# Adding two decay tiles with an accumulating transfer instead of a VectorE instruction

## The chip, the core and the metric

The kernel runs on one core of one Trainium2 chip. The core has engines with an instruction queue each: TensorE (PE, matrix products, its weight loads shown as PEld), VectorE (DVE), ScalarE (ACT), GpSimd (POOL) and SyncE (SP), which here only issues transfers. An engine takes its instructions in order; an instruction that waits for something holds up all that stands behind it on that engine. Transfers run on 16 DMA engines that all issuers share. The metric is the device time of one execution in microseconds (us), lower is better. Before the change the median of three runs is 1244.33 us (1241.67 to 1247.54).

## What is computed

The reference is one layer of a hybrid block over 512 latent tokens of width 1024, with a context of 256 tokens. An input projection feeds a convolution branch and a bidirectional state-space mixer (Mamba-2, chunked scan with chunks of 128 tokens, 32 heads in 8 groups of 4, state 128), the branches are gated and projected, and a squared-ReLU MLP follows. What matters here is the part of the scan inside a chunk, once forwards and once on the flipped sequence:

```python
cum = jnp.cumsum(dts * a, axis=2)
seg = cum_t[..., :, None] - cum_t[..., None, :]
decay = jnp.exp(jnp.where(lower, seg, -jnp.inf))
cb = jnp.einsum('bcqgn,bckgn->bcgqk', cs_, bs)
y_diag = jnp.einsum('bcgrqk,bckgrp->bcqgrp', cb[:, :, :, None] * decay, xdt)
...
y = y_f + flip(y_b) + lp['ssm_d'][:, None] * xs
```

Both directions multiply the same product `cb` of C and B, so the kernel adds the forward decay (a lower triangle) and the backward decay (an upper triangle) of a head first, and multiplies the sum by `cb` once.

## The kernel before

Weights arrive as 128x1024 tiles `raw` (three buffers, SP issues them, L100); ACT rounds each to `whi` (L109) and DVE makes the rest `wlo` (L110). A projection tile is 24 matmuls of 512 columns (L118 to L120: three products for each of 8 slices). The program has an opening (norms, modulation, first projections), the scan stage with a loop over the 8 groups, and then gates, output projections and the MLP.

In the scan stage `ssd(g)` does the scan of group g while `proj(g + 1)` computes the next group's B, C, X and Z tiles, and for the first five groups a GLU tile and its 31-tap convolution on DVE (`taps`, L601) is mixed in. The list of instructions on each engine is fixed when the program is built: a list scheduler takes instructions by priority and by its own estimate of when each operand is ready, so an operation that moves to another engine moves others as well.

Per head, `expo` (L450) makes the summed decay two heads ahead of its use. For each direction it loads one row of cumulated sums from DRAM (`s_cf`), spread over 128 partitions, into a tile E of 128x512 float32 (L459, issued by SP, 256 KB); POOL masks one triangle (L463, affine select); ACT exponentiates in four pieces (L466). The forward tile comes from a pool with seven buffers and is freed when PE has used the product. The backward tile comes from tag "M" with three buffers; its last reader is the addition of both tiles (L468), which frees it for the backward tile of three heads later. DVE multiplies the sum by `cb` (L551), and PE uses it in the third part of `yps` (L560). The first two parts of `yps` (L564) need C times the decay from the chunk's start: tiles Cd, loaded by SP (L482) and multiplied on POOL, one in four on DVE (L483), and the states `hst`, which DVE steps from chunk to chunk (L541, L542) out of `sps` products (L529) of `xw` (L514). Then DVE forms `yt` (L568, L569), ACT stores it and squares it, and POOL sums the squares (`yacc`, L574).

SP's one queue thus carries the weights, the E rows and the Cd rows, in the scheduler's order.

Of the kernel before, what the change touches and what calls it, by code (L numbers as in the profile page):

```python
# [12 lines left out]
ALU = mybir.AluOpType  # L13
# [47 lines left out]
def build(tc, xT, ctxT, cond, crow, wada1, wada2, vecs, hv, cst, w_in, w_co, w_so, w_o, w_1, w_2, outT):  # L61
    nc = tc.nc
    with ExitStack() as es:
# [386 lines left out]
        def expo(upto):  # L450

            while asked[0] < min(upto, HEADS):
                h = asked[0]
                asked[0] += 1
                es_ = []
                for d in range(2):
                    hd = d * HEADS + h
                    e = (tp if d else spool).tile([P, T], F32, name="E", tag="M" if d else "E", bufs=3 if d else EB)
                    nc.sync.dma_start(e, s_cf[hd, 0].unsqueeze(0).broadcast_to([P, T]))  # L459

                    x3 = e.rearrange("p (c q) -> p c q", q=P)
                    sign = -1 if d else 1
                    nc.gpsimd.affine_select(x3, x3, pattern=[[0, NCH], [sign, P]], compare_op=ALU.is_ge,  # L463
                                            fill=never, base=0, channel_multiplier=-sign)
                    for c in range(NCH):
                        nc.scalar.activation(x3[:, c], x3[:, c], AF.Exp, bias=bT[:, c, hd:hd + 1])  # L466
                    es_.append(e)
                nc.vector.tensor_tensor(es_[0], es_[0], es_[1], ALU.add)  # L468
                ahead.append(es_[0])

        def ssd(g, Bt, Ct, X, Z):
# [72 lines left out]
            for j in range(2):  # L544
# [4 lines left out]
                for r in range(2):  # L549
                    M = ahead.pop(0)  # L550
                    nc.vector.tensor_tensor(M, M, cb, ALU.mult)  # L551
                    Ms.append(M)
                expo(4 * g + 2 * j + 2 + LEAD)
                for k in range(3):
                    for c in range(NCH):
# [53 lines left out]
        conv = first_xbc[0]  # L609
        cur = proj(0)  # L610
        expo(2)
        for g in range(G):
            ssd(g, *cur)
# [289 lines left out]
```

## Time and profile before

| | |
|---|---|
| median of the runs | 1244.33 us (1241.67 to 1247.54) |
| the profiled execution's own time | 1247.21 us |
| its span, first to last instruction | 1245.4 us |
| granted TensorE clock, mean | 0.991 |
| busy: PE, DVE, ACT, POOL | 1202.5, 919.3, 565.8, 166.7 us |
| E tiles loaded, additions of two E tiles | 64, 32 |

Busy time is the time in which an engine has an instruction running; the share over the whole span mixes stages that differ, so the stages are read apart. A wait is listed with the engine and line that waits, the one that ended it, the sum in us, how often, and the longest. In a timeline a row is start, duration, engine, line, operation, and how many instructions were merged; SPq and ACTq are transfers as they are issued. "To landing" is the time from the issue of a transfer to its arrival. L468 runs only in the scan stage, between 115.9 and 528.5 us of the span.

### The profile page before, as it was taken

Reading aid. Unit: us, or ns where it says so; the run is one execution under the profiler, and the core shown is the slowest. Engines: PE = TensorE matmul, PEld = TensorE weight load, DVE = VectorE, ACT = ScalarE, POOL = GpSimd, SP = SyncE. Lnnn points to the kernel's source line nnn. Section 1 sums busy time; section 2 is a strip of 40 time slices with the busy share of each in tenths; the row PEclk is TensorE's granted clock in tenths of the full one; section 3 lists DMA queues with packets and bytes.
Section 4 is the critical chain, followed back from the end, with each engine's and each line's share of the span. In section 5 each row is a group of like instructions: output and inputs, shape, how many; then the busy total and the mean of one; then the engine's idle time right before and its main releaser. Section 6 shows DMA issues by size and latency. Waiting matters only on the chain.

```text
span 1245.4 us, 17389 instructions
## 1 busy us (share of the span) xinstructions
PE 1202.5 (97%) x6662; PEld 996.3 (80%) x6662; DVE 919.3 (74%) x1426; ACT 565.8 (45%) x916; POOL 166.7 (13%) x138
## 2 busy tenths in 40 slices
PE   6998999999999999999999999999999999999997
PEld 3787778788888887787887878789988888888886
DVE  6797889999999989866999698877733343443454
ACT  4557877465564635342453561234422332322342
POOL 0003725042242424120010000000000000000000
PEclk8999999999999999999999999999999999999998
DMA  9427853443525352422363468956013332332322
GB/s 366 159 65 162 259 156 125 126 147 101 186 85 178 105 167 76 126 78 94 111 184 111 128 201 282 315 165 193 35 44 92 102 92 95 102 91 96 102 85 68
DMA packets 65331, 169.83 MB, mean 136 GB/s; under 512 B 7648, under 2 KB 10464, under 8 KB 65120
## 3 DMA queue, kind: packets, MB, share of 16 engines
q1 hardware_dynamic: 62944, 164.53, 42.1%
q10 hardware_dynamic: 2304, 4.20, 0.9%
q8 instruction: 52, 0.85, 0.3%
q14 instruction: 31, 0.25, 0.1%
HBM read 162.14 MB, written 6.55 MB: 135 GB/s over the span
## 4 chain that ended last, share of the span: by engine, by line
PE 64%; DVE 11%; DMA 9%; ACT 3%; issue 2%; POOL 0%; SPq 0%; DVEq 0%; POOLq 0%; ACTq 0%
PE ps L118 19%; PE ps L120 19%; PE ps L119 19%; DVE conv L601 3%; DMA E<-s_cf 3%; DMA Cd<-s_cf 3%; PE sps L529 2%; DMA aw<-in_wada_dram 2%; DVE wlo L110 2%; ACT E L466 2%; PE yps L564 2%; DMA yr<-s_y 1%; DVE Xt L381 1%; DVE Ct L381 1%; DVE Cd L483 1%
## 5 line engine op out<-in xcount | busy, mean ns | idle before, releaser
L109 ACT CAST whi<-raw 128x1024 fp32r<-128x1024 f32 x163 | 170.9, 1049 | 349.7 <-PE ps L119 304.4
L110 DVE TENSOR_TENSOR wlo<-raw,whi 128x1024 fp32r<-128x1024 f32 x163 | 202.2, 1241 | 97.5 <-ACT whi L109 89.0
L120 PE MATMUL ps<-hh,wlo 128*128 128x512 f32 x632 | 255.7, 405 | 4.2 <-DVE wlo L110 4.2
L118 PE MATMUL ps<-hh,whi 128*128 128x512 f32 x632 | 255.3, 404 | 3.2 <-DVE Ct L381 2.4
L119 PE MATMUL ps<-hl,whi 128*128 128x512 f32 x632 | 253.9, 402 | 0.0
L601 DVE SCALAR_TENSOR_TENSOR conv<-sg,V,conv 128x392 f32<-128x392 f32 (+14 forms) x240 | 177.2, 755 | 2.2
L120 PEld LDWEIGHTS ps<-hh,wlo 128*128 128x128 f32 x632 | 118.8, 188 | 33.9 <-DVE wlo L110 8.6
L118 PEld LDWEIGHTS ps<-hh,whi 128*128 128x128 f32 x632 | 118.8, 188 | 30.1 <-issue 5.9
L119 PEld LDWEIGHTS ps<-hl,whi 128*128 128x128 f32 x632 | 119.0, 188 | 25.3 <-issue 1.4
L738 DVE SCALAR_TENSOR_TENSOR x<-ps,mod,x 128x512 f32<-128x512 f32 (+1 forms) x48 | 31.6, 661 | 98.8 <-PE ps L120 98.8
L466 ACT ACTIVATE E<-E,bT 128x128 f32<-128x128 f32 x256 | 81.6, 394 | 34.3 <-POOL E L463 34.1
L120 PE MATMUL ps<-h2h,wlo 128*128 128x512 f32 (+1 forms) x240 | 89.9, 376 | 0.0
L119 PE MATMUL ps<-h2l,whi 128*128 128x512 f32 (+1 forms) x240 | 89.7, 375 | 0.0
L118 PE MATMUL ps<-h2h,whi 128*128 128x512 f32 (+1 forms) x240 | 89.7, 376 | 0.0
L119 PE MATMUL ps<-gl,whi 128*128 128x512 f32 x224 | 88.4, 395 | 0.0
L118 PE MATMUL ps<-gh,whi 128*128 128x512 f32 x224 | 88.2, 394 | 0.0
L120 PE MATMUL ps<-gh,wlo 128*128 128x512 f32 x224 | 87.9, 392 | 0.0
L463 POOL TENSOR_SCALAR_AFFINE_SELECT E<-E 128x512 f32<-128x512 f32 x64 | 51.9, 821 | 231.9 <-DVE Bt L381 102.2
L483 POOL TENSOR_TENSOR Cd<-Ct,Cd 128x512 f32<-128x512 f32 x48 | 76.8, 1630 | 40.5 <-ACT Ct L391 33.9
L381 DVE SCALAR_TENSOR_TENSOR Xt<-ps,V,Xt 128x510 f32<-128x510 f32 (+3 forms) x128 | 74.3, 605 | 5.5 <-ACT Xt L377 5.1
L118 PE MATMUL ps<-hc,whi 128*128 128x256 f32 x184 | 52.2, 283 | 1.4 <-DVE Xt L381 1.4
L120 PE MATMUL ps<-hc,wlo 128*128 128x256 f32 x184 | 52.2, 284 | 0.0
(260 smaller groups left out, 2307.6 us busy)
## 6 DMA issues: line engine op xcount, KB each, us to landing
raw<-in_w_in_dram SPq DMA_DIRECT2D x81, 512.0 KB, 3.7
raw<-in_w_dram SPq DMA_DIRECT2D x64, 512.0 KB, 3.6
E<-s_cf SPq DMA_DIRECT2D x64, 256.0 KB, 5.5
Cd<-s_cf SPq DMA_DIRECT2D x64, 256.0 KB, 5.1
aw<-in_wada_dram SPq DMA_DIRECT2D x64, 256.0 KB, 4.0
ablk<-in_wada_dram SPq DMA_DIRECT2D x16, 512.0 KB, 7.3
raw<-in_w_so_dram SPq DMA_DIRECT2D x16, 512.0 KB, 3.7
s_y<-yt ACTq DMA_DIRECT2D x16, 256.0 KB, 5.1
```

Source lines behind the costliest of these rows:

```text
L109: nc.scalar.copy(hi, raw)
L110: nc.vector.tensor_tensor(lo, raw, hi, ALU.subtract)
L118: nc.tensor.matmul(ps, lhsT=whi[:, k, :], rhs=rhi[:, k, t0:t1], start=start and k == 0, stop=False)
L119: nc.tensor.matmul(ps, lhsT=whi[:, k, :], rhs=rlo[:, k, t0:t1], start=False, stop=False)
L120: nc.tensor.matmul(ps, lhsT=wlo[:, k, :], rhs=rhi[:, k, t0:t1], start=False, stop=stop and k == KT - 1)
L381: nc.vector.scalar_tensor_tensor(o[:, lo:hi], ps[:, lo + d:hi + d], vcol(V_SCW + 5 * ch + j), o[:, lo:hi], ALU.mult, ALU.add)
L463: nc.gpsimd.affine_select(x3, x3, pattern=[[0, NCH], [sign, P]], compare_op=ALU.is_ge, fill=never, base=0, channel_multiplier=-sign)
L466: nc.scalar.activation(x3[:, c], x3[:, c], AF.Exp, bias=bT[:, c, hd:hd + 1])
L483: (nc.vector if (d, r) in DECAYS_V else nc.gpsimd).tensor_tensor(Cd, Ct, Cd, ALU.mult)
L529: nc.tensor.matmul(ps[:, d * 256:(d + 1) * 256], lhsT=ch(Bk, c), rhs=xw[d][:, wi[d](c)].rearrange("p h e -> p (h e)"), start=i == 0, stop= ...
L601: nc.vector.scalar_tensor_tensor(o[:, :, lo:hi], u[:, :, lo + d:hi + d], wv(j), o[:, :, lo:hi], ALU.mult, ALU.add)
L738: nc.vector.scalar_tensor_tensor(x1[:, j, a:b], ps[:, a:b], mod[:, gcol + j, 0:1], x1[:, j, a:b], ALU.mult, ALU.add)
```

## The change

The addition of the backward tile to the forward one is no longer a VectorE instruction. It is a transfer from SBUF to SBUF, issued from the GpSimd queue, that adds its source to what is in the destination:

```diff
@@ -465,7 +465,7 @@
                     for c in range(NCH):
                         nc.scalar.activation(x3[:, c], x3[:, c], AF.Exp, bias=bT[:, c, hd:hd + 1])
                     es_.append(e)
-                nc.vector.tensor_tensor(es_[0], es_[0], es_[1], ALU.add)
+                nc.gpsimd.dma_start(es_[0], es_[1], accum_op=ALU.add)
                 ahead.append(es_[0])
```

The 32 additions go from DVE's list, 32 transfers come into POOL's, and the scheduler places them and what depends on them anew. In the rows below the number behind a name is the number of the tile's buffer generation: E_928 and E_935 are the forward and backward tile of the first head, E_943 and E_950 of the second, then 1039/1046, 1054/1061, 1113/1120, 1128/1135, 1660/1667, 1675/1682, 1736/1743, 1751/1758, 2283/2290; the backward tiles share three buffers, so 1061 takes the place of 935, 1120 of 950, 1135 of 1046, and so on. Behind "waits" stand the semaphores: DMAHW for transfers issued by SP and ACT, DMASW for those from POOL.

First place: POOL in the first group, from the second half of that group's Cd products on. Before:

```order
L483 TENSOR_TENSOR Cd_1099<-Ct_590,Cd_1099 128x512 [waits DMAHW1_49,PE_49]
L483 TENSOR_TENSOR Cd_1102<-Ct_590,Cd_1102 128x512 [waits DMAHW2_49]
L483 TENSOR_TENSOR Cd_1108<-Ct_590,Cd_1108 128x512 [waits DMAHW3_49]
L463 AFFINE_SELECT E_1113<-E_1113 128x512 [waits DMAHW4_49]
L463 AFFINE_SELECT E_1061<-E_1061 128x512 [waits DMAHW6_49,DVE_49]
L463 AFFINE_SELECT E_1128<-E_1128 128x512 [waits DMAHW7_49]
```

The same place with the change:

```order
L483 TENSOR_TENSOR Cd_1099<-Ct_590,Cd_1099 128x512 [waits DMAHW1_49,PE_49]
L468 DMA E_928<-E_935 128x512 [waits Activation_49,Pool_49]
L483 TENSOR_TENSOR Cd_1102<-Ct_590,Cd_1102 128x512 [waits DMAHW2_49]
L483 TENSOR_TENSOR Cd_1108<-Ct_590,Cd_1108 128x512 [waits DMAHW3_49]
L463 AFFINE_SELECT E_1113<-E_1113 128x512 [waits DMAHW4_49]
L468 DMA E_943<-E_950 128x512 [waits Activation_49,Pool_49]
L463 AFFINE_SELECT E_1128<-E_1128 128x512 [waits DMAHW6_49]
L463 AFFINE_SELECT E_1061<-E_1061 128x512 [waits DMAHW0_49,DMASW0_49]
L468 DMA E_1039<-E_1046 128x512 [waits Activation_49,Pool_49]
L463 AFFINE_SELECT E_1660<-E_1660 128x512 [waits DMAHW2_49]
L463 AFFINE_SELECT E_1120<-E_1120 128x512 [waits DMAHW3_49,DMASW1_49]
L468 DMA E_1054<-E_1061 128x512 [waits Activation_49,Pool_49]
```

The transfer of the first head stands behind the first Cd product, and the transfer of the third head behind the mask of E_1061, a tile that can only be loaded when the first transfer has landed.

Second place: POOL in the second group, with the change (before, the additions of heads 1660, 1675 and 1736 were on DVE and no mask stood ahead of them there):

```order
L574 TENSOR_TENSOR yacc_584<-yacc_584,ysq_1170 128x512 [waits Activation_49]
L463 AFFINE_SELECT E_1736<-E_1736 128x512 [waits DMAHW1_49]
L463 AFFINE_SELECT E_1743<-E_1743 128x512 [waits DMAHW2_49,DMASW5_49]
L463 AFFINE_SELECT E_1751<-E_1751 128x512 [waits DMAHW3_49,PE_49]
L463 AFFINE_SELECT E_2283<-E_2283 128x512 [waits DMAHW7_49,PE_49]
L468 DMA E_1660<-E_1667 128x512 [waits Activation_49,Pool_49]
L463 AFFINE_SELECT E_1758<-E_1758 128x512 [waits DMAHW2_49,DMASW6_49]
L468 DMA E_1675<-E_1682 128x512 [waits Activation_49,Pool_49]
L468 DMA E_1736<-E_1743 128x512 [waits Activation_49,Pool_49]
L463 AFFINE_SELECT E_2290<-E_2290 128x512 [waits DMAHW4_49,DMASW7_49]
L468 DMA E_1751<-E_1758 128x512 [waits Activation_49,Pool_49]
```

Transfers and masks now alternate, and the masks of E_1758 and E_2290 wait for the transfer just ahead of them.

Third place: SP at the end of the second group, where E rows, weights and Cd rows share the queue. Before:

```order
L100 DMA raw_1971<-in_w_in_dram 128x1024 [waits DMAHW7_49,DMAHW2_49,DVE_49]
L459 DMA E_1758<-s_cf_578 128x512 [waits DMAHW3_49,DVE_49]
L459 DMA E_2290<-s_cf_578 128x512 [waits DMAHW5_49,DMAHW4_49,DVE_49]
L459 DMA E_2305<-s_cf_578 128x512 [waits DMAHW5_49,DVE_49]
L459 DMA E_2366<-s_cf_578 128x512 [waits DMAHW6_49,DMAHW3_49,DVE_49]
L482 DMA Cd_1728<-s_cf_578 128x512 [waits PE_49]
L100 DMA raw_2039<-in_w_in_dram 128x1024 [waits DMAHW0_49,DVE_49]
```

With the change:

```order
L459 DMA E_1758<-s_cf_578 128x512 [waits DMAHW2_49,DMASW6_49,Pool_49]
L100 DMA raw_1971<-in_w_in_dram 128x1024 [waits DMAHW6_49,DMAHW3_49,DVE_49]
L459 DMA E_2290<-s_cf_578 128x512 [waits DMAHW4_49,DMASW7_49,Pool_49]
L459 DMA E_2305<-s_cf_578 128x512 [waits DMASW0_49,DMAHW5_49,Activation_49,Pool_49]
L459 DMA E_2366<-s_cf_578 128x512 [waits DMASW1_49,DMAHW2_49,Activation_49,Pool_49]
L482 DMA Cd_1728<-s_cf_578 128x512 [waits DMAHW7_49,PE_49]
L482 DMA Cd_2202<-s_cf_578 128x512 [waits DMAHW0_49,PE_49]
L100 DMA raw_2039<-in_w_in_dram 128x1024 [waits DMAHW1_49,DVE_49]
```

The four E loads waited for DVE and now wait for POOL's transfers; Cd_1728 and raw_2039 stay behind them.

## Prediction

> **What bounds the kernel now.** First the stages: the view of busy time by stretch (columns: the stretch in us of the span, its length, busy us and instructions of PE, PEld, DVE, ACT and POOL, clock, share of the DMA engines, GB/s).
>
> ```profile
> 100.00:150.00 50.00, 43.73 (x286) 35.84 (x285) 40.74 (x61) 39.69 (x83) 29.93 (x27) 0.97 0.83 219
> 150.00:580.00 430.00, 417.22 (x2581) 347.36 (x2580) 384.02 (x551) 237.12 (x433) 127.00 (x104) 1.00 0.41 127
> 580.00:860.00 280.00, 278.81 (x1240) 227.55 (x1239) 239.96 (x391) 113.49 (x144) 9.54 (x4) 1.00 0.59 188
> 860.00:1200.00 340.00, 339.83 (x1692) 287.21 (x1691) 152.88 (x219) 108.10 (x149) 0.00 (x0) 1.00 0.29 88
> ```
>
> The scan stage is 100 to 580. From 580 on PE has work nearly all the time and nothing of the change runs there. In the scan stage PE is still the bound: it idles 6.3 us in the first stretch and 12.8 us in the second. DVE, which loses work, is busy 384 of 430 us there, so it is close behind. All that the change can win is in these 19.1 us. Which of them DVE could give back, the list of waits of PE says (waiter, releaser, sum, times, longest; this stage alone), with one wait of DVE's own:
>
> ```profile
> PE yps L564 <- DVE Cd L483: 6.3, 8, 1.5
> PE ps L120 <- DVE wlo L110: 3.4, 5, 1.0
> PE sps L529 <- DVE xw L514: 3.1, 2, 2.5
> PE ps L118 <- DVE Ct L381: 2.4, 4, 1.5
> DVE Cd L483 <- DMA Cd<-s_cf: 10.4, 9, 3.6
> ```
>
> The largest is no fault of DVE's: DVE itself waits 10.4 us for those Cd rows. The next three, 8.9 us, are DVE being late.
>
> **What is removed.** By the line:
>
> ```profile
> L468 DVE TENSOR_TENSOR E<-E x32: 675/679/1116, 115.9 to 528.5; 128x512 f32<-128x512 f32 x32
> ```
>
> 32 additions of 0.68 us (the median of three durations in ns: least, median, most), 21.8 us of DVE. The first 8 belong to the first two groups, which another cost governs (below); the other 24 free 16.3 us over some 380 us, 4%. Of the 8.9 us of PE's waits for a late DVE I count a third, **-3 us**; it could be 0, and at most all 8.9.
>
> **What is added: the transfer itself.** No transfer of this form is in the trace. Nearest are transfers of 256 KB (operation, KB each, median us from issue to landing; then least, median, most of the E loads; the page's busy times; one issue on SP):
>
> ```profile
> E<-s_cf SPq DMA_DIRECT2D x64, 256.0 KB, 5.5
> s_y<-yt ACTq DMA_DIRECT2D x16, 256.0 KB, 5.1
> out_dram<-x SPq DMA_DIRECT2D x8, 256.0 KB, 2.4
> DMA to landing us min/median/max: 3.0/5.5/10.5
> PE 1202.5 (97%) x6662; PEld 996.3 (80%) x6662; DVE 919.3 (74%) x1426; ACT 565.8 (45%) x916; POOL 166.7 (13%) x138
> 383.60 0.38 SPq L482 DMA_DIRECT2D Cd<-s_cf  x1
> ```
>
> I take a = 5.1 us, that of s_y<-yt: same size, read from SBUF, in the same stage. Below stands 2.4 us, a store at the quiet end; above 10.5 us, the longest E load, since an addition must also read its destination. What POOL itself spends on the issue is unknown too: an issue on SP takes 0.38 us, POOL's product on a tile 1.6 us (4.72/3 below); even 32 x 1.6 = 51 us would leave POOL, busy 166.7 us, far from full, and I count it within a.
>
> The Trainium skill (DMA: Bandwidth & Descriptors, "Anatomy of one DMA") fits a transfer issued from GpSimd as 2.0 us plus bytes over 436 GB/s, which for 256 KB makes an estimate of 2.6 us. It is no row of this case; by it the sum below would come out near zero, which is the first rival.
>
> **What is moved: the order on POOL and SP.** The addition ended the life of the backward tile, one of three buffers. Now the next backward tile's load waits on SP for the landing, its mask on POOL waits for that load, and the scheduler has put the next transfer behind this mask. That makes a chain in which each link is a transfer, a load and a mask. In the opening of the scan it has no head start. The rows of before that it is made of, from the page's groups (busy us, mean ns, idle time ahead), the timelines of POOL and DVE and the chain of waits (start, us, what):
>
> ```profile
> L463 POOL TENSOR_SCALAR_AFFINE_SELECT E<-E 128x512 f32<-128x512 f32 x64 | 51.9, 821 | 231.9 <-DVE Bt L381 102.2
> 122.73 4.72 POOL L483 TENSOR_TENSOR Cd<-Ct,Cd 128x512 f32<-128x512 f32 x3 [1.57 <-DMA Cd<-s_cf]
> 146.71 4.78 POOL L483 TENSOR_TENSOR Cd<-Ct,Cd 128x512 f32<-128x512 f32 x3
> 151.44 2.29 POOL L574 TENSOR_TENSOR yacc<-yacc,ysq 128x512 f32<-128x512 f32 x1
> 153.67 2.40 POOL L463 TENSOR_SCALAR_AFFINE_SELECT E<-E 128x512 f32<-128x512 f32 x4
> 116.64 0.69 DVE L551 TENSOR_TENSOR E<-E,cb 128x512 f32<-128x512 f32 x1
> 132.17 3.34 DMA Cd<-s_cf
> 139.69 1.06 PE yps L560 x14
> 175.36 3.88 DMA Cd<-s_cf
> 180.01 1.85 PE yps L564 x29
> ```
>
> Start: the first transfer stands behind the first of three Cd products on POOL, 122.73 + 4.72/3 = 124.3. A mask is 0.82 us (mean of 64, 821 ns), a load I take as b = 4.5 us, between the lone Cd load at 132.17 (3.3) and the median of 5.5, because the chain spreads the loads out. Then, all in series:
>
> - transfer 928, load and mask of E_1061; transfer 1039, load and mask of E_1135; transfer 1113, load and mask of E_1682;
> - on POOL, ahead of the transfer of 1660, three Cd products (4.78), one yacc (2.29) and four masks (2.40);
> - transfer 1660, load and mask of E_1758; transfer 1675, load and mask of E_2290; transfer 1751; only then SP passes E_2366 and issues Cd_1728.
>
> That is 6a + 5b + 5 x 0.82 + 9.47 = 30.6 + 22.5 + 13.6 = 66.7 us, so Cd_1728 is issued at 191.0. Before it was issued at 175.36, and PE's yps at 180.01 waited for it and for nothing later. The delay there is **+15.6 us**.
>
> On the way half of it is already lost in the first group: the product by cb of the first head ran at 116.64 and can now run at 124.3 + 5.1 = 129.4 at the soonest, with the steps of hst queued behind it on DVE; and SP passes E_1135 (waiting for transfer 1039, 140.1) before Cd_1105, which makes yps of the second pair end about 8 us after its 140.75 (139.69 + 1.06). The products by cb of heads 1660 and 1675 then hold up xw and hst. I do not add these: they lie ahead of the same end.
>
> **The later groups hide it.** From the fourth group on the loads start early enough. Rows of one such group, from the timelines:
>
> ```profile
> 395.35 1.63 POOL L463 TENSOR_SCALAR_AFFINE_SELECT E<-E 128x512 f32<-128x512 f32 x2 [1.77 <-DMA E<-s_cf]
> 396.01 2.46 ACT L466 ACTIVATE E<-E,bT 128x128 f32<-128x128 f32 x8 [3.17 <-POOL E L463]
> 407.90 1.28 ACT L466 ACT_TABLE_LOAD   x1 [1.92 <-DMA E<-s_cf]
> 412.88 9.82 POOL L483 TENSOR_TENSOR Cd<-Ct,Cd 128x512 f32<-128x512 f32 x6 [4.29 <-ACT Ct L391]
> 416.55 0.33 SPq L100 DMA_DIRECT2D raw<-in_w_in_dram  x1
> 429.97 1.05 ACT L109 CAST whi<-raw 128x1024 fp32r<-128x1024 f32 x1 [2.86 <-PE ps L119]
> 435.10 3.58 DVE L551 TENSOR_TENSOR E<-E,cb 128x512 f32<-128x512 f32 x4
> 448.45 1.06 PE yps L564 x16
> ```
>
> The group's first transfer can go at 397.0 (end of the two masks) and lands at 402.1; load 4.5, mask 0.8, exponentials 2.5 (four of eight, and a table load of 1.28), next transfer 5.1: 415.0. The weight load behind it on SP went at 416.55 before, so it is not late; the products by cb start at 435.10, 20 us later. After one more load and mask, at 420.3, POOL makes six Cd products (9.8 us, before at 412.88), ready at 430 for yps at 448.45. With a = 10.5 it would go some 10 us late (two transfers of +5.4, less the 1.5 in hand). The weight issued at 416.55 is rounded at 429.97 and takes about 4 us to land, so some 9 us are spare: even then little is lost. So 0 here.
>
> **Sum.** 1247.21 (the profiled execution) + 15.6 - 3 = 1259.8. That execution lies 2.9 us above the median of the runs, so on the median's scale **1257 us**, +1.0%.
>
> **Rivals.**
>
> *The transfers are short and nothing moves.* With a = 2.4 the chain gives 15.6 - 6 x 2.7 = -0.6, no delay at its end; left are some 3 us in the first group (yps needs hst, hst stands behind a product that waits until 126.7), against 3 gained: **1244 us**. For it: the store of 2.4 us. Against: the DMA engines are busy 83% from 100 to 150.
>
> *Slower still.* An addition reads two tiles and writes one; at 1.5 times s_y<-yt, a = 7.7, and loads of 5.5: 15.6 + 6 x 2.6 + 5 x 1.0 = 36 us, less 3: **1277 us**. For it: the crowded stretch, and each link enters six times. Against: the chain itself thins the traffic.
>
> *Faster.* The delayed start is absorbed (a under 2.4, loads near their least of 3.0) and DVE's relief reaches PE whole, 8.9 us: **1235 us**. The mechanism is that DVE, 89% busy, sets when wlo, xw and Ct are ready. For it: those three rows. Against: PE idles only 12.8 us in 430.
>
> *The change does less than it says:* the addition leaves DVE, but DVE stands at the product by cb for the landing, so that its 21.8 us come back as waits. This would show in the first two groups only and is in the forecast there.
>
> **How the numbers follow.** The forecast (1251 to 1266) gets 0.48, the slower one 0.20, no change 0.20, faster 0.12. A change under 0.5%, about 6 us, can't be told from none here: 1238 to 1250.5 is the same. So slower 0.68, same 0.20, faster 0.12. The range, 1240 to 1280 us, takes in the cost of a from 2.4 to nearly 8 and leaves out the far ends (a = 10.5 would give 15.6 + 32.4 + 5 - 3 = +50, 1294 us).
>
> **What would show it.** Right: L468 on POOL's queue with landings near 5 us; PE idle between 120 and 205 up by about 15 us, ended by yps, xw or hst, with DVE waiting for a transfer at L551 there; the Cd load of the second group issued near 191; from 250 on no idle time of PE for L551. Wrong: landings of 2 to 3 us and the same Cd load before 180 (then no loss), or waits of PE for wlo in every group (then weights are late behind the E loads, and the loss repeats five times). The chain's order is read from the queues, so if its links overlap after all, the delay shrinks by whole links of about 10 us.

## The result

After the change the median of four runs is 1280.45 us (1279.09 to 1287.8), against 1245.17 us for the kernel before on the same chip: ratio 1.0285, 95% interval 1.0261 to 1.031. So the change costs 35 us. The prediction was 1257 us, slower with a chance of 0.68: the direction was right, the size was not.

The profiled execution took 1279.24 us, its span is 1277.5 us (before 1245.4). The view of busy time by stretch, for the first two stretches of the prediction:

```profile
100.00:150.00 50.00, 37.21 (x239) 29.54 (x238) 28.55 (x47) 31.97 (x74) 23.74 (x27) 0.86 0.83 187
150.00:580.00 430.00, 401.73 (x2416) 336.78 (x2416) 357.60 (x504) 238.23 (x428) 155.03 (x135) 0.98 0.50 145
```

PE idles 12.8 us in the first stretch (6.3 before) and 28.3 us in the second (12.8 before). The granted clock, 0.97 and 1.00 before, is 0.86 and 0.98. DVE has lost its additions, 357.6 us of busy time against 384.0, and nothing came of it. The transfers themselves (durations in ns of the issue on POOL; then least, median, most from issue to landing in us; then the E loads of this kernel):

```profile
L468 POOL DMA_DIRECT2D E<-E x32: 852/865/1189, 123.7 to 555.8; - x32
DMA to landing us min/median/max: 3.3/3.9/10.1
E<-s_cf SPq DMA_DIRECT2D x64, 256.0 KB, 5.0
```

Where in the scan the time went is read from the start of the second yt of each group (L569 on DVE), which ends the group:

| end of group | 0 | 1 | 2 | 3 | 4 | 5 | 6 | 7 |
|---|---|---|---|---|---|---|---|---|
| before, us | 143.1 | 185.5 | 253.7 | 321.7 | 390.5 | 460.3 | 524.5 | 579.3 |
| after, us | 151.2 | 196.0 | 270.9 | 342.6 | 415.0 | 488.3 | 554.7 | 610.7 |
| delay so far | 8.0 | 10.6 | 17.2 | 21.0 | 24.5 | 28.0 | 30.2 | 31.4 |

The opening (groups 0 and 1) loses 10.6 us. The rest, 20.8 us, is lost in the later groups, 6.6 us in group 2 and 1 to 4 us in each of the others, where the prediction had put nothing. Groups 2 to 7 as two stretches, before and then after:

```profile
185.46:579.25 393.79, 382.15 (x2347) 318.76 (x2346) 356.16 (x516) 208.44 (x364) 114.33 (x91) 1.00 0.40 122
```

```profile
196.04:610.67 414.63, 389.65 (x2357) 325.57 (x2356) 348.29 (x494) 213.29 (x366) 134.33 (x112) 0.98 0.45 130
```

Of the 20.8 us, 13.3 are idle time of PE (25.0 against 11.6) and 7.5 are PE being busy longer with the same work, at the lower clock. What PE waits for in the later groups (220 to 560 us), before and after:

```profile
PE yps L564 <- DVE Cd L483: 4.0, 5, 1.5
PE ps L118 <- DVE Ct L381: 2.4, 4, 1.5
```

```profile
PE ps L118 <- DVE Ct L381: 12.8, 4, 3.8
PE yps L564 <- DVE Cd L483: 4.0, 5, 1.1
PE ps L118 <- ACT E L466: 2.7, 1, 2.7
```

The first matmul of a projection waits until DVE has read an older projection (Ct) out of PSUM. The Ct tile leaves PSUM by two readers: an instruction on ACT (L377, here called its eviction) and four steps on DVE (L381). How the wait comes about is seen around 356 us of the changed kernel: the timelines of ACT, DVE and PE, one after the other.

```profile
356.11 1.28 ACT L466 ACTIVATE E<-E,bT 128x128 f32<-128x128 f32 x4 [3.52 <-POOL E L463]
357.30 1.03 ACT L109 CAST whi<-raw 128x1024 fp32r<-128x1024 f32 x1
358.24 0.77 ACT L377 ACTIVATE Ct<-ps,V 128x512 f32<-128x512 f32 x1
...
358.37 1.22 DVE L110 TENSOR_TENSOR wlo<-raw,whi 128x1024 fp32r<-128x1024 f32 x1 [2.79 <-ACT whi L109]
363.42 0.74 DVE L381 SCALAR_TENSOR_TENSOR Ct<-ps,V,Ct 128x510 f32<-128x510 f32 x1
...
364.31 0.77 PE L118 MATMUL ps<-hh,whi 128*128 128x512 f32 x1 [2.58 <-DVE Ct L381]
364.87 0.63 PE L119 MATMUL ps<-hl,whi 128*128 128x512 f32 x1
367.40 0.40 PE L119 MATMUL ps<-hl,whi 128*128 128x512 f32 x1
```

ACT stands 3.52 us at the exponentials of a backward tile whose mask (L463) is late. Behind them in its list stand a weight rounding (whi, L109) and the eviction of Ct (L377). DVE waits for whi, its four steps on Ct come late, and PE stands 2.58 us. Then PE's clock is down as well: the matmuls after the gap take 0.63 us each, and 0.40 from 367.40 on. The same place before:

```profile
327.28 2.45 ACT L466 ACTIVATE E<-E,bT 128x128 f32<-128x128 f32 x8 [2.53 <-POOL E L463]
329.63 0.55 ACT L377 ACTIVATE Bt<-ps,V 128x256 f32<-128x256 f32 x1
331.02 2.45 ACT L466 ACTIVATE E<-E,bT 128x128 f32<-128x128 f32 x8
333.37 1.04 ACT L109 CAST whi<-raw 128x1024 fp32r<-128x1024 f32 x1
334.31 0.77 ACT L377 ACTIVATE Ct<-ps,V 128x512 f32<-128x512 f32 x1
```

Exponentials stood ahead of whi and Ct before, too, only nothing held them there. ACT did wait for masks before the change: from 220 to 560 us 26.3 us in all, against 21.6 after it. But its eight waits of over 2 us stood ahead of the Bt eviction or of the squares of yt, as the first rows show, and none of PE's waits at L118 was longer than 1.5 us. After the change a wait of 3.2 to 3.9 us stands ahead of whi and the Ct eviction in each of the groups 3 to 6 (at 284, 356, 428 and 502 us), and each is followed some 8 us later by a gap of PE of 2.6 to 3.7 us. So what grew is not the time that ACT waits for masks; it is what stands behind the wait.

### The profile page after: what moved, and what is told of

Read it like the earlier page. It is cut to its first block, busy times and chain, and to the rows that moved or that the text cites. A ratio compares the mean times of both kernels' runs of the same rounds, so it can differ in the third digit from the quotient of the medians.

```text
span 1277.5 us, 17440 instructions
## 1 busy us (share of the span) xinstructions
PE 1211.9 (95%) x6662; PEld 1004.2 (79%) x6662; DVE 901.2 (71%) x1394; ACT 567.7 (44%) x916; POOL 189.9 (15%) x170
## 4 chain that ended last, share of the span: by engine, by line
PE 64%; DMA 14%; DVE 14%; issue 3%; ACT 3%; POOL 1%; SPq 1%; DVEq 0%; POOLq 0%; ACTq 0%
PE ps L118 19%; PE ps L120 19%; PE ps L119 19%; DMA E<-s_cf 4%; DVE conv L601 4%; DMA Cd<-s_cf 3%; DMA E<-E 3%; PE sps L529 2%; DVE wlo L110 2%; DMA aw<-in_wada_dram 2%; DVE Xt L381 2%; DMA yr<-s_y 2%; PE yps L564 2%; DVE Ct L381 1%; POOL E L463 1%
## 5 line engine op out<-in xcount | busy, mean ns | idle before, releaser
L109 ACT CAST whi<-raw 128x1024 fp32r<-128x1024 f32 x163 | 170.9, 1049 | 364.0 <-PE ps L119 319.9
L118 PE MATMUL ps<-hh,whi 128*128 128x512 f32 x632 | 259.0, 410 | 16.9 <-DVE Ct L381 12.8
L120 PE MATMUL ps<-hh,wlo 128*128 128x512 f32 x632 | 259.4, 410 | 3.7 <-DVE wlo L110 3.6
L119 PE MATMUL ps<-hl,whi 128*128 128x512 f32 x632 | 257.3, 407 | 0.0
L118 PEld LDWEIGHTS ps<-hh,whi 128*128 128x128 f32 x632 | 121.2, 192 | 43.7 <-ACT Xt L377 9.5
L118 PE MATMUL ps<-h2h,whi 128*128 128x512 f32 (+1 forms) x240 | 89.8, 376 | 0.0
L118 PE MATMUL ps<-gh,whi 128*128 128x512 f32 x224 | 88.3, 394 | 0.0
L381 DVE SCALAR_TENSOR_TENSOR Xt<-ps,V,Xt 128x510 f32<-128x510 f32 (+3 forms) x128 | 74.9, 606 | 7.8 <-ACT Xt L377 7.2
L463 POOL TENSOR_SCALAR_AFFINE_SELECT E<-E 128x512 f32<-128x512 f32 x64 | 50.7, 799 | 184.6 <-DMA E<-s_cf 181.3
L564 PE MATMUL yps<-Cd,hst 128*64 128x128 f32 x512 | 37.3, 286 | 18.2 <-DVE Cd L483 10.0
L118 PE MATMUL ps<-hc,whi 128*128 128x256 f32 x184 | 52.3, 284 | 1.4 <-DVE Xt L381 1.4
```

Of the source, the lines that this page charges most:

```text
L109: nc.scalar.copy(hi, raw)
L118: nc.tensor.matmul(ps, lhsT=whi[:, k, :], rhs=rhi[:, k, t0:t1], start=start and k == 0, stop=False)
L119: nc.tensor.matmul(ps, lhsT=whi[:, k, :], rhs=rlo[:, k, t0:t1], start=False, stop=False)
L120: nc.tensor.matmul(ps, lhsT=wlo[:, k, :], rhs=rhi[:, k, t0:t1], start=False, stop=stop and k == KT - 1)
L381: nc.vector.scalar_tensor_tensor(o[:, lo:hi], ps[:, lo + d:hi + d], vcol(V_SCW + 5 * ch + j), o[:, lo:hi], ALU.mult, ALU.add)
L564: nc.tensor.matmul(o, lhsT=hst[:, s, k, hr * 64:hr * 64 + 64], rhs=ch(Cs[k][r], c), start=k == 0 and c == 0, stop=False, skip_group_check= ...
```

## The experiments

In this part "opening" is the time until the end of group 1 and "groups 2 to 7" the time from there to the last yt; both are from the profiled execution, the medians from all runs. Before has 185.5 and 393.8 us, after 196.0 and 414.6. The profiled execution of before took 1247.2 us, the medians of before beside the experiments are 1242 to 1244, so differences of medians come out 3 to 5 us larger than those of profiles. An order edge (`tc.issue_after` in the cuts from the code) tells the scheduler to put one instruction behind another on its engine. The scheduler then places other instructions anew as well, so no run here changes one queue alone.

**Where the loss sits.** Two halves of the change, each with VectorE's addition for the other heads; the diff is that of the late half, the early half has the two branches exchanged:

```diff
-                nc.gpsimd.dma_start(es_[0], es_[1], accum_op=ALU.add)
+                if h < 8:
+                    nc.vector.tensor_tensor(es_[0], es_[0], es_[1], ALU.add)
+                else:
+                    nc.gpsimd.dma_start(es_[0], es_[1], accum_op=ALU.add)
```

> Heads 0 to 7 (the first two groups and the head start) use the transfer, heads 8 to 31 the VectorE addition as before. Theory S (two separate losses: the chain in the opening costs 10.6 us by the milestones of yt, each later group 2 to 7 us by a cause of its own, 20.8 us in all): 1245 + 10.6 = 1256 us, between 1252 and 1260, and groups 3 to 7 have the length that they have before the change (68 to 70 us). Rival R (there is one loss: the opening has used up the head start of the E loads, and the later groups run late only because of it): near 1275 us, and the later groups stay 3 us longer each. The prediction's own step (later groups cost 0) gives 1257 us here as for the whole change.

Measured: 1256.51 us (1253.09 to 1259.18), ratio to before 1.0107 (1.0077 to 1.0137). Groups 2 to 7 take 394.2 us, as before; the opening ends at 192.1, 6.6 us late. This is inside theory S's interval, and the later groups are no longer than before, against rival R.

> The mirror image: VectorE adds for heads 0 to 7, the transfer for heads 8 to 31. Theory S: the opening is as before, the later groups lose what they lost with the whole change, 1245 + 20.8 = 1266 us, between 1259 and 1269 (part of the 6.6 us lost in the third group may be inherited from the opening). Rival R: the head start is kept, so no loss: 1242 to 1249 us. The prediction's steps give 1245 - 2 = 1243 us here.

Measured: 1272.58 us (1270.58 to 1275.64), ratio 1.024 (1.0211 to 1.027). The opening ends at 182.0, earlier than before; groups 2 to 7 take 420.3 us. Groups 3 to 7 take 341.0 us (339.7 with the whole change, 325.5 before). So the later loss does not need a late opening: rival R falls, and there are two losses, as theory S has it. But they don't simply add up: the time is above the bound of 1269 us, and group 2 alone took 79.3 us (74.9 with the whole change). There the timelines of POOL, ACT, DVE and PE show the same event in a larger size, and a second one:

```profile
208.23 7.76 POOL L486 TENSOR_TENSOR Cd<-Ct,Cd 128x512 f32<-128x512 f32 x6
215.68 0.90 POOL L463 TENSOR_SCALAR_AFFINE_SELECT E<-E 128x512 f32<-128x512 f32 x1
...
216.61 0.40 ACT L466 ACTIVATE E<-E,bT 128x128 f32<-128x128 f32 x1 [4.94 <-POOL E L463]
216.92 0.76 ACT L377 ACTIVATE Xt<-ps,V 128x512 f32<-128x512 f32 x1
...
209.32 8.35 DVE L110 TENSOR_TENSOR wlo<-raw,whi 128x1024 fp32r<-128x1024 f32 x1
...
219.20 0.77 PE L118 MATMUL ps<-hh,whi 128*128 128x512 f32 x1 [5.87 <-DVE Xt L381]
```

A mask that missed its turn stands behind six Cd products, the exponential behind the mask, and an Xt eviction behind the exponential. At the same time one wlo on DVE lasted 8.35 us (median 1.22), as long as POOL's products went on, and DVE's steps on Xt stood behind it. Both waits end at about 217.6; how much of the 5.87 us is due to which can't be told from this trace.

**Is ACT's queue the place?** One order edge per group, put on ACT's list alone: the exponentials of one backward tile go behind the eviction of Ct (`evicted` holds the eviction of each tile; here and below the lines that note such an instruction are left out of the cut).

```diff
-                    for c in range(NCH):
-                        nc.scalar.activation(x3[:, c], x3[:, c], AF.Exp, bias=bT[:, c, hd:hd + 1])
+                    held = d and h % 4 == 2 and h > 8
+                    with tc.issue_after(evicted[24 + h // 4 - 1].ins) if held else nullcontext():
+                        for c in range(NCH):
+                            nc.scalar.activation(x3[:, c], x3[:, c], AF.Exp, bias=bT[:, c, hd:hd + 1])
```

> The change, with one order edge per group on ScalarE: the exponentials of one backward tile (head 4g+2), which stand ahead of a weight rounding (L109) and of the Ct eviction (L377), are put behind that eviction. No other engine's work is altered. Theory Q (ScalarE's queue: these exponentials wait for a late mask and hold the rounding and the eviction, TensorE then lacks a free PSUM tile and stands 2.6 to 3.8 us, with a lower granted clock behind it): the stalls of TensorE at L118 in five groups (15.5 us of waits against 2.4 before) go to under 4 us in all, and the time falls by 11 to 18 us, to 1262 to 1270 us. Rival W (weights: SyncE stands 54 us at E loads whose buffer waits for a landing, and weight loads queue behind them): the rounding is late because raw is, the edge changes nothing, 1278 to 1283 us. Rival P (GpSimd: 0.87 us per issue delays masks and Cd products): no change either.

Measured: 1282.18 us (1280.1 to 1283.58), ratio 1.0314 (1.0288 to 1.034). No gain, so by what was written this speaks for W or P. (The scheduler did move others' work: POOL's list differs from 213 us on, DVE's from 228 on.) The waits of PE from 220 to 560, and two stalls, on ACT and PE, and on POOL, DVE and PE:

```profile
PE ps L118 <- DVE Xt L383: 13.2, 5, 4.6
PE ps L118 <- DVE Ct L383: 4.9, 1, 4.9
```

```profile
307.61 0.70 ACT L470 ACTIVATE E<-E,bT 128x128 f32<-128x128 f32 x2 [5.69 <-POOL E L465]
310.37 0.55 ACT L379 ACTIVATE Xt<-ps,V 128x256 f32<-128x256 f32 x1
...
312.23 0.47 PE L118 MATMUL ps<-hh,whi 128*128 128x512 f32 x1 [2.22 <-DVE Xt L383]
```

```profile
372.05 7.81 POOL L487 TENSOR_TENSOR Cd<-Ct,Cd 128x512 f32<-128x512 f32 x6
...
374.32 7.22 DVE L110 TENSOR_TENSOR wlo<-raw,whi 128x1024 fp32r<-128x1024 f32 x1
...
383.07 0.76 PE L118 MATMUL ps<-hh,whi 128*128 128x512 f32 x1 [4.59 <-DVE Xt L383]
```

At 312 us the stall had not gone, it had moved: from Ct to the next eviction, that of Xt, which now stood behind the held exponentials. The gaps at 383 and 457 us (4.59 and 4.54) are another matter: the Xt eviction on ACT had run at 376.22, ahead of the held exponentials, but a wlo on DVE lasted 7.2 us beside POOL's six Cd products, and the steps on Xt stood behind it. At 221 us the Ct eviction stands behind exponentials without an edge, and PE waits 4.91 us. One edge was too little to test the theory. The next run puts the exponentials of all backward tiles from head 10 on behind the last X eviction of their group:

```diff
-                    held = d and h % 4 == 2 and h > 8
-                    with tc.issue_after(evicted[24 + h // 4 - 1].ins) if held else nullcontext():
+                    held = d and h >= 10
+                    with tc.issue_after(evicted[2 * ((h - 2) // 4 - 1) + 1].ins) if held else nullcontext():
```

> The change, with order edges on ScalarE that put the exponentials of every backward tile from head 10 on behind the last X eviction of the group in which they run, so that none can hold an eviction or a weight rounding of B, C and X; the run with one tile moved had shown the same exponentials holding the next eviction (Xt) instead. Theory Q (ScalarE's queue is where the late mask becomes a loss): TensorE's waits at L118 from 220 to 560, 16.3 us with the change and 18.1 with one tile moved, fall under 5 us, and the groups 3 to 6 shorten from 72 to 73 us to under 70.5: 1258 to 1268 us, if the chain of loads, now later, doesn't reach the products by cb. If Q is wrong: stalls at L118 remain and 1278 us or more.

Measured: 1256.46 us (1252.53 to 1256.98), ratio 1.0095 (1.0068 to 1.0121); 24 us better than the change alone and a little under the interval written. PE's waits from 220 to 560, and groups 2 to 7 as one stretch:

```profile
PE yps L568 <- DVE Cd L487: 2.8, 5, 0.8
PE ps L120 <- DVE wlo L110: 2.6, 4, 0.7
PE sps L533 <- DVE xw L518: 1.8, 1, 1.8
```

```profile
194.11:585.40 391.29, 382.69 (x2357) 321.31 (x2356) 345.30 (x494) 212.38 (x366) 133.95 (x112) 1.00 0.48 137
```

No wait for an eviction is left among those listed, and groups 2 to 7 take 391.3 us at a clock of 1.00, where before has 393.8. The transfers, their landings and POOL's issues are all still there, and SP still waits for landings with its E loads (61.8 us from 220 to 560, 54.2 without the edges). ACT's waits for masks of over 2 us stand ahead of the Bt eviction and the squares again, where before has them. So the loss of the later groups passes through ACT's queue: theory Q holds, and neither W nor P, the time that the issues take, is enough to make it. One thing is not separated: with the edges the scheduler also put the last of a group's four transfers behind the six Cd products on POOL (in group 3 the products start at 283 and the transfer goes at 296; without the edges all four go ahead of them). What is left is 13.3 us by the medians and 9.1 by the profiles, where the opening is 8.7 us longer (it ends at 194.1), groups 2 to 7 are 2.5 shorter, and the stretch behind them is 2.9 longer.

Two controls: the kernel before with the same edges, and the late half of the change with them.

> Control: the kernel before with the same order edges on ScalarE, the addition on VectorE for all heads. It tells whether the edges alone win, so that the transfer has no part in a gain. If the relief of VectorE is worth something in the later groups (they took 67.5 to 68.3 us with transfers and edges, 68.9 to 69.7 before): no gain here, 1241 to 1250 us. If the edges are what shortens those groups: 1234 to 1241 us.

Measured: 1243.91 us (1241.3 to 1247.84), ratio 1.001 (0.9998 to 1.0023). The edges alone win nothing.

> VectorE adds for heads 0 to 7, transfers from head 8 on, and the order edges on ScalarE from head 10 on (backward exponentials behind the last X eviction of their group). With these edges groups 2 to 7 took 391.3 us for the whole change, against 393.8 before, and heads 0 to 7 on VectorE gave an opening 3.5 us shorter than before. Theory S + Q (two separate losses, each mended by its own means): the two add up, 1235 to 1244 us, at or below the time before. If the losses hang together (the head start is used up in another way): 1250 us or more.

Measured: 1244.21 us (1239.82 to 1246.02), ratio 1.0012 (1.0 to 1.0025). With the opening left to VectorE and ACT's queue cleared, 24 of the 32 transfers cost nothing that can be measured, and they win nothing either: with 16 us less work on DVE the time is 0.3 us longer than that of the control, with an uncertainty of nearly 2 us. That is net; what the transfers cost and what the relief gives are not told apart. It lies just above the interval that was expected, 1235 to 1244.

**What makes the mask late?** First the landing that frees the backward tile. It was taken away by letting the transfer read a constant, and put into the kernel before by a transfer that only copies the tile to DRAM; then a fourth buffer lets each load wait for an earlier transfer; then the addition is an instruction on GpSimd, with no landing at all.

```diff
-                nc.gpsimd.dma_start(es_[0], es_[1], accum_op=ALU.add)
+                nc.gpsimd.dma_start(es_[0], V[:, :T], accum_op=ALU.add)
```

> The change, but each transfer reads a constant tile (the first 512 columns of the table of vectors) in place of the backward tile; the backward decay is left out of the sum. Size, issuer, number and landing of the transfers and VectorE's relief stay, but the backward tile is free as soon as its exponentials are done, not when the transfer has landed. Theory L (the landing that releases the backward tile makes load, mask and exponentials late, and these hold evictions on ScalarE): the loss goes, 1238 to 1252 us, no wait of TensorE at L118 over 2 us from 220 to 560. Rivals P (0.87 us of GpSimd per issue) and D (the traffic of 32 more transfers): 1268 us or more. In between, 1255 to 1265, if the forward half (the product by cb waiting for the landing) matters in the opening.

Measured: 1261.27 us (1260.05 to 1264.72), ratio 1.0147 (1.0125 to 1.0169), above the 1252 us of theory L, in its middle case, and under the rivals' 1268. Half of the loss is gone: groups 3 to 7 take 321.4 us (325.5 before the change, 339.7 after), although the transfers stand in POOL's queue as with the change. The rest lies in the opening, which ends at 193.4 because the first product by cb still waits 13.2 us for a landing and PE 10.9 for hst, and in group 2, which took 77.1 us (68.3 before). Its trace shows the same event once more: a mask behind six Cd products, ACT waiting 5.51 us for it at 226.60 with the Xt eviction behind, and PE 2.61 us at 232.16. That is only a part of the 8.8 us.

```diff
                 nc.vector.tensor_tensor(es_[0], es_[0], es_[1], ALU.add)
+                nc.gpsimd.dma_start(s_e[h], es_[1])
```

> The reverse: the kernel before, VectorE's addition kept, and one transfer more per head from GpSimd's queue that only copies the finished backward tile to a DRAM buffer nobody reads. VectorE isn't relieved and the sum is ready as early as before; only the release of the backward tile now waits for a landing. Theory L: most of the loss comes back with the addition still on VectorE, 1262 to 1285 us, with TensorE waiting at L118 for evictions in each group. Rival F (what costs is that the sum itself is late for the product by cb): 1243 to 1252 us.

Measured: 1253.12 us (1251.02 to 1255.04), ratio 1.0076 (1.0055 to 1.0097). This is under theory L's interval and 1 us above rival F's. Groups 2 to 7 take 393.5 us, as before; the loss is in the opening, which ends at 189.0. But in the later groups the run did not do what it was made for. The copy is issued when the exponentials are done and lands in 2.5 us (median), and VectorE's addition comes later: of the 29.4 us that E loads wait for a copy's landing, 28.5 lie before 200 us, and from 220 to 560 they wait for the addition, 17.6 us, as before (18.9). So it says nothing against theory L there. In the opening, where the landing did come last, there is a loss, but also an hst step on DVE that lasted 3.72 us (median 0.69) beside POOL's Cd products.

```diff
-CDB, EB, LEAD = 5, 7, 2
+CDB, EB, LEAD = 5, 6, 2
-            return tp.tile([P, n], dt, name=name, tag="M", bufs=3)
+            return tp.tile([P, n], dt, name=name, tag="M", bufs=4)
-                    e = (tp if d else spool).tile([P, T], F32, name="E", tag="M" if d else "E", bufs=3 if d else EB)
+                    e = (tp if d else spool).tile([P, T], F32, name="E", tag="M" if d else "E", bufs=4 if d else EB)
```

> The change, with four buffers for the backward tile instead of three and six for the forward tile instead of seven. A backward tile's load then waits for the landing of the transfer four heads earlier, not three. If the loss comes from loads and masks that wait for a landing (theories S and Q together): most waits of SyncE for a landing (54 us from 220 to 560) go, the opening has one more head before the chain closes, and the time falls to 1250 to 1265 us. If the transfers' traffic on the DMA engines or GpSimd's time for issuing them is the cause: no gain, 1278 us or more. If the sixth forward buffer less is what decides: above 1282 us.

Measured: 1275.41 us (1267.44 to 1283.54, four runs wide apart), ratio 1.0283 (1.0238 to 1.0327). The profiled one, of 1267.44 us, has groups 2 to 7 at 401.1 us (two thirds of the later loss gone) and an opening that ends at 198.6, later still. By its median it meets no expectation. Nor did the waits go that it was to take away: SP still waits 49.6 us for landings from 220 to 560 (54.2 with the change). It settles nothing.

```diff
-                nc.gpsimd.dma_start(es_[0], es_[1], accum_op=ALU.add)
+                nc.gpsimd.tensor_tensor(es_[0], es_[0], es_[1], ALU.add)
```

> The addition as an instruction of GpSimd in place of the transfer: the same queue, no landing, VectorE relieved alike. GpSimd's product on a tile takes 1.3 to 1.6 us, against 0.87 us of issue and 3.9 us to landing. Theory L: the backward tile is released 3 us sooner than with the transfer, so most of the loss goes, 1246 to 1260 us. Rival P (the place in GpSimd's queue, where the addition waits for exponentials and holds masks and Cd products): the loss stays, 1272 us or more, since GpSimd is busy longer per addition.

Measured: 1272.63 us (1270.18 to 1274.55), ratio 1.0233 (1.0211 to 1.0254), rival P's interval: without any landing most of the loss is there. Theory L had counted on a release 3 us sooner. It isn't sooner: SP's own waits from 220 to 560 for whatever frees the backward tile are, in the kernel before, with the change, with the constant as source, with the copy beside VectorE's addition, and with POOL's addition:

```profile
SPq L459 <- DVE E L468: 18.9, 14, 4.7
SPq L459 <- DMA E<-E: 54.2, 14, 8.1
SPq L459 <- ACT E L466: 22.7, 10, 12.0
SPq L460 <- DVE E L469: 17.6, 14, 4.2
SPq L459 <- POOL E L468: 48.0, 14, 8.3
```

The second and the last, where the load waits about 50 us for the release, lose some 13 us or more in groups 3 to 7 (339.7 and 338.5 us against 325.5); the other two with transfers lose nothing there (321.4 and 326.0).

> The addition as an instruction of GpSimd (1272.6 us without edges), now with the edges on ScalarE that put the exponentials of the backward tiles from head 10 on behind the last X eviction. Theory Q (what costs in the later groups is whatever makes the mask late, through ScalarE's queue, and not the transfer as such): its waits of TensorE for evictions at L118 (13.4 us from 220 to 560) go, groups 2 to 7 shorten from 409.6 us to under 395, 1250 to 1259 us. If GpSimd's own load is what costs there: 1266 us or more.

Measured: 1259.45 us (1258.96 to 1263.11), ratio 1.0131 (1.0108 to 1.0155), 0.45 us above the upper bound of theory Q. Groups 2 to 7 go from 409.6 to 399.6 us (not under 395), which is 10.0 of the 15.8 us that they had lost. PE's list has no wait at L118 for DVE any more (11.2 and 2.2 us without the edges); 3.5 us at L118 for ACT are left, in four waits of at most 0.9. So the same edges mend the larger part where there is no transfer. Taken together, what the losing kernels share is a late release of the backward tile, by a landing or by an instruction behind others in POOL's queue; the loss arises where the late load, mask and exponentials then stand ahead of an eviction on ACT. The runs agree on this, but each also moved other instructions, so the first link, from the release to the mask, is argued from five kernels and not isolated by one.

**The opening.** DVE's first product by cb waits for the first transfer, and hst stands behind it (waits of DVE and PE from 100 to 150 in the changed kernel, and the Cd load of the second group on SP):

```profile
DVE E L551 <- DMA E<-E: 11.1, 2, 8.8
PE yps L564 <- DVE hst L542: 8.2, 1, 8.2
```

```profile
176.68 8.85 SPq L459 DMA_DIRECT2D E<-s_cf  x3
185.63 0.87 SPq L482 DMA_DIRECT2D Cd<-s_cf  x2
```

With the edges on ACT kept, the product was put behind the last step of hst:

```diff
-                    nc.vector.tensor_tensor(M, M, cb, ALU.mult)
+                    with tc.issue_after(last_hst.ins) if g < 2 else nullcontext():
+                        nc.vector.tensor_tensor(M, M, cb, ALU.mult)
```

> Transfers for all heads, the edges on ScalarE, and in the first two groups edges on VectorE that put the product by cb behind the last step of hst. With the edges on ScalarE alone the opening still lost 8.7 us; VectorE stood 8.9 us at the first product by cb for the first transfer's landing, hst behind it, and TensorE waited 8.3 us for hst. Theory V (the opening, too, is lost in an engine's queue: the waiting product holds hst): the wait of TensorE for hst falls under 2 us and the time goes to 1246 to 1251 us. The prediction's theory (the chain of six transfers, loads and masks sets the end of the opening through Cd of the second group): the first group is shorter, but the end of the second stays, 1254 to 1259 us.

Measured: 1254.86 us (1250.44 to 1259.0), ratio 1.0097 (1.0077 to 1.0118). PE's wait for hst is 1.1 us, as theory V has it, but the time is that of the prediction's theory. The next wait took its place (100 to 200 us):

```profile
PE yps L569 <- DVE Cd L487: 7.2, 1, 7.2
```

The Cd row of the second pair stands behind E loads on SP that wait for landings. The kernel before with both kinds of edges, as a control:

> Control for the run with both kinds of edges: the kernel before with both, addition on VectorE. If the edges only mend what the transfer broke, 1241 to 1250 us, as before. If they help by themselves, below 1240 us. The difference to the run with transfers is what the transfer is worth once nothing stands behind its landing: VectorE's relief (theory: 2 to 5 us in favour of the transfer in the later groups) less the opening.

Measured: 1242.98 us (1239.86 to 1245.97), ratio 1.0001 (0.999 to 1.0013): no effect. Last, six backward loads were put behind the Cd loads that they held up, for all heads with transfers:

```diff
-                    nc.sync.dma_start(e, s_cf[hd, 0].unsqueeze(0).broadcast_to([P, T]))
+                    first = cd_load.get(0 if h in (4, 5) else 1 if h in (9, 10, 11, 12) else None)
+                    with tc.issue_after(first.ins) if d and first else nullcontext():
+                        nc.sync.dma_start(e, s_cf[hd, 0].unsqueeze(0).broadcast_to([P, T]))
```

> Transfers for all heads, the edges on ScalarE and VectorE as in the run with both, and one more set on SyncE: the loads of the backward tiles of heads 4, 5 and 9 to 12, which wait for landings, are put behind the Cd load of the first and of the second group that stood behind them. With both edges the first group still lost time, no longer to hst (1.1 us) but to Cd (7.2 us in one wait), and the second group's Cd was issued at 184 us against 175 before. The prediction's step (the chain on SyncE sets the end of the opening, through Cd): these waits shrink to under 3 us, yt of the second group comes at 186 to 190 us instead of 194.3, and the time falls from 1254.9 to 1245 to 1251 us. Rival (the opening is bound by the decays themselves, whose products by cb then come late): the wait moves on to the product by cb, 1253 to 1258 us.

Measured: 1260.37 us (1254.46 to 1266.55), ratio 1.0131 (1.0091 to 1.0172). It lies above both intervals, and the profiled execution, 1266.55 us, is the longest of its four. In it the first group ends at 143.8 us, as before the change (143.1), so its 8 us were the two queues, DVE's and SP's; but the second group ends at 196.0. What PE waits for longest between the two is in neither theory: a wlo on DVE lasts 5.59 us, again beside POOL's Cd products.

```profile
154.12 4.30 POOL L492 TENSOR_TENSOR Cd<-Ct,Cd 128x512 f32<-128x512 f32 x3
...
153.93 5.59 DVE L110 TENSOR_TENSOR wlo<-raw,whi 128x1024 fp32r<-128x1024 f32 x1
...
159.57 0.80 PE L120 MATMUL ps<-hh,wlo 128*128 128x512 f32 x1 [4.61 <-DVE wlo L110]
```

So this run does not tell whether the second group could be mended. No order tried ends it as early as before with transfers for all heads; only VectorE's addition there does. No version was found that beats the kernel before.

## Why the prediction was right and wrong

**The bound, and DVE's relief: half right.** PE is the bound and its idle time tells the loss. The relief was put at -3 us out of 8.9; what was measured is 0: transfers for 24 heads and VectorE's addition for all, with the same edges, differ by 0.3 us (1244.21 and 1243.91, uncertain by nearly 2 us). PE's waits for a late wlo, xw, Bt, Ct or Xt from 100 to 600 us are as long with the transfers as without (7.7 and 7.8 us), so the freed time did not reach them.

**The price of the transfer: too high.** a = 5.1 us was taken, 3.9 is measured (3.3 to 10.1). The loads, b = 4.5, took 5.0 in the median. POOL's issue takes 0.865 us, inside the bounds that were left. The estimate of 2.6 us beside it was too low.

**The chain in the opening: right, with those sizes.** It was 6a + 5b + 13.6 us from 124.3, which puts Cd_1728 at 191.0. With the measured a and b it is 124.3 + 23.4 + 25.0 + 13.6 = 186.3; that row stands above, at 185.63. That the sum comes so near is in part luck: the links differ from the medians (the first transfer took 6.5 us to land, the last two loads 3.4 and 3.7), and POOL's work ahead of the fourth transfer took 11.3 us in place of 9.47. But the transfer of 1660, due at 165.0 by the forecast's terms, went at 165.44. The first product by cb was to run at 129.4 at the soonest and ran at 130.26; the first group was to be 8 us late and is 8.0 (the 140.1 on the way to it is 139.8 by the terms given). The end of the opening, +15.6 in the forecast, is +10.6, because a was taken too high; PE's idle time between 120 and 205 us grew by 8.9 us, not by 15.

**"The later groups hide it": this step failed: put at 0, it measured 20.8 us.** It asked of two things whether they come late: the weight loads behind the E loads on SP, and the products by cb. Both were answered rightly: from 220 to 560 PE waits for wlo 2.3 us, 2.4 before, and no wait of PE for a product by cb is listed there. What was not asked is what stands behind the exponentials on ACT. The rows quoted there already showed ACT waiting 3.17 us for POOL's mask, and the whi rounding on the same engine; that wait stood ahead of the Bt eviction and did no harm, and the change brought one like it ahead of whi and the Ct eviction. The step added up the way of one tile to its own use, 20 us later, and found it free; the harm was to another tile's work that shares a queue with it.

The Trainium skill (TensorE: Matmul & The Clock Gate, "Architectural detail", the paragraph on engine queue depths) calls ACT and DVE strictly first in, first out. The traces agree: at 356 us exponentials that waited 3.52 us held whi and Ct, and with one edge, at 307.61, exponentials that waited 5.69 us held the Xt eviction behind them. It stood open to the prediction, which used the rule for SP, POOL and DVE, but not for ACT.

**The clock: not in the sum at all.** It is 7.5 of the 20.8 us, the time that PE is busy longer with the same work.

**The rivals.** The slower one, 1277 us, is nearest by its number, for a wrong reason: its transfers were to take 7.7 us. The change's own sign of being wrong, waits of PE in every group so that the loss repeats, was named, but with the weights as the way, not the evictions. The range of 1240 to 1280 us took its upper end from the price of a alone and missed by 0.45 us.

**What stays open:** whether a landing alone, with nothing else moved, brings the later loss: the run made for it did not delay the release in the later groups. A part of group 2 with the constant as source, and what the second group of the opening would need, are not explained either.

## What to carry to other kernels

A result that is late but has slack can still cost time: look behind every instruction that would wait for it, on each in-order engine, not only at who uses it. When an order edge makes a stall jump to the next instruction of the same engine, suspect the queue, look at the trace of each stall, and put the whole set of waiting instructions behind the work that they hold. An experiment that delays something has to be read in its own trace: here the copy that was to delay a release did so only in the opening. Work taken off an engine that is 89% busy was worth nothing here, as PE's waits for that engine did not get shorter.

## What the hardware showed that was not expected

A short stall of PE is paid twice. The windows around the stall at 362 us:

```profile
360.00:364.00 4.00, 1.73 (x15) 1.52 (x13) 4.00 (x7) 3.97 (x7) 1.56 (x3) 0.99 0.85 198
364.00:368.00 4.00, 3.69 (x10) 2.98 (x11) 4.00 (x8) 3.97 (x7) 0.00 (x0) 0.58 0.27 67
```

After a gap of 2.58 us the granted clock was 0.58 over the next 4 us. Seven matmuls from 364.31 to 367.40 took 3.09 us, 0.44 each, where they start every 0.23 us at full clock: 1.5 us on top of the 2.58. In the opening, after the 8.2 us for hst, the clock was 0.80 over the whole stretch from 125 to 150:

```profile
125.00:150.00 25.00, 15.16 (x122) 11.68 (x122) 14.99 (x24) 13.44 (x32) 12.73 (x15) 0.80 0.76 180
```

The Trainium skill (TensorE: Matmul & The Clock Gate, "HAM oscillation — how this bites in real kernels") says to leave no gap of more than about 3.4 us, as PE then restarts at half clock. The trace agrees on the half clock, and differs on the gap: 2.58 us were enough here, and the measurement decides; one of 2.72 us in another group (at 436.58) cost no clock.

A DVE instruction can last several times its usual length beside a row of POOL's Cd products: wlo 8.35, 7.22, 7.20 and 5.59 us (median 1.22) in the runs above, each ending 1.1 us after the end of one of POOL's products or masks. In the kernels before and after no wlo lasted over 2.3 us, though the same products run there. What decides between the two was not tested.

The third surprise is small: an accumulating transfer of 256 KB, which reads two tiles and writes one, lands in 3.9 us in the median, sooner than the E loads of the same size (5.0).
